# Compressed rows split ahead of a gate quarter and expanded behind it, and query pieces asked for five ahead

## The chip, the core and the metric

The kernel runs on one core of a Trainium2 chip. The metric is the device time of one execution in microseconds. Three runs of the kernel before took 1874.07, 1874.98 and 1877.89 us; the median is 1874.98.

## The reference

The reference is a two-layer backbone over 1024 latent tokens and 256 context tokens, 1024 wide, in float32. The even layer has four differential-attention heads and eight heads of multi-head latent attention, the odd layer a bidirectional mLSTM and neighbourhood attention. The change touches the even layer's projection and the start of its attention:

```python
z = jnp.einsum('bsd,de->bse', h, w_in) + b_in
q1, q2, k1, k2, v, cq, ckv, k_rope, gate = split_cols(z, EVEN_SPLIT)
...
qm = to_heads(jnp.einsum('bsr,re->bse', rms_norm(cq, q_norm_g), w_uq), MLA_HEADS)
kvm = to_heads(jnp.einsum('bsr,re->bse', rms_norm(ckv, kv_norm_g), w_ukv), MLA_HEADS)
q_nope, q_rope = qm[..., :MLA_NOPE], qm[..., MLA_NOPE:]
k_nope, vm = kvm[..., :MLA_NOPE], kvm[..., MLA_NOPE:]
...
y = jnp.concatenate([from_heads(oa), from_heads(ob)], axis=-1) * jax.nn.silu(gate)
```

So 256 columns of `z` are the compressed queries, 128 the compressed keys and values and 32 the rotary part of the keys. They are normalised by rows and expanded by `w_uq` and `w_ukv`. A further 1024 columns are the gate.

## The kernel before

A token group `TG` is four tiles of 128 tokens, four more, and the two tiles of context. A float32 product is made of three: each operand is split into a rounded high part and the rest, and `product` (L434 to L436) adds high by high, high by low and low by high in one PSUM bank. `parts` (L452, L453) makes such a split of a result: ScalarE writes the high part `eh`, VectorE the low part `el`, and each has two buffers. A buffer is free again when its store has landed.

The projection stage ends with this sequence. The 416 compressed columns are made for all tiles (L1270 on, the tile `cz`). Then `compressed(t0, n)` does for one group, in this order: the norms on GpSimd (L1291, L1296), the rotation of the key part, the transposes (L1306) and their splits into `cq` and `ck` (L1309, L1310), the rotary key part with its store to `s_kr` (L1317), four blocks of expanded keys with two stores each to `s_mk` (L1325), six blocks of expanded queries whose stores go to `s_mq` (L1338), and one block of values for each tile, stored to `s_mv` (L1360). A query block of the first four holds two heads and takes four stores; each of the last two holds sixteen columns of all eight heads and takes sixteen. All stores and loads are issued by SyncE's queue, one behind the other.

`gate(j)` makes a quarter of the gate: 256 columns for all three groups, 24 matmuls to a bank, a SiLU on ScalarE into the tile `e` (two buffers, shared with the values and the rotation), and a store (L1375). When it begins it takes its split weights, and at the same moment asks for the next quarter's (`next(w0)`, load L363, split L383 and L391, one staging buffer `raw`).

The four tiles of banks "tr" belong to the compressed rows, the four banks "mm" to the gate. Outside the parts that are marked as manual, the order of the instructions on each engine is set when the program is built: among those that are estimated to be ready, the one that stands earlier in the text goes first. So the order of the text gives precedence, and work from further on fills in.

When the pool `cp` of the compressed rows (it holds `uq`, `wu`, `cz`, `cq`, `ck`) is closed, the pool `a0` is opened on the same side of the memory, and the first attention unit's tiles are loaded into it: 24 loads of L590 to L592 for queries and keys, one for values (L597), one for the gate (L599). `gate(3)` stands behind that.

The attention has a plan written out by hand: each task has an engine, an estimated cost, the tasks before it, and the buffers that it takes and gives; `Plan.run` picks the task that can start earliest among the next 99. `Latent.shifts` adds the rough scores that give each row's maximum ahead of the latent heads (L858): for each head, nine steps of one or two tiles, which read query pieces of 256 tokens, `rq`, five buffers, loaded by L850. The key tiles for them go into the weight ring (L844, L845). One step goes behind each of the 36 blocks of the differential heads, and the rest are spread over the latent heads. In the kernel before, the load of a piece is added to the plan in the step that first uses it.

Of the kernel before, what the change touches and what calls it, by code (L numbers as in the profile page):

```python
# [19 lines left out]
P = 128  # L20
D = 1024
# [33 lines left out]
RQ = 5  # L55
# [146 lines left out]
def hybrid_kernel(ctx, tc, t, out, dbg=None):  # L202
# [253 lines left out]
    def keys_of(tt):  # L456
        k0 = 0 if tt < LT else LT
        return k0, NT - k0 * P
# [78 lines left out]
    def on_vector(n):  # L537
        return fixed["V"] + n / 960

    def on_scalar(n, act=True):  # L540
        return fixed["act" if act else "copy"] + n / 1200
# [10 lines left out]
                self.load_scores(pool, b)  # L552
            self.load_values(pool)

    spare, stored = {}, []

    def moves(plan, bank, dst, m, last, cut=3):

# [12 lines left out]
    def taken(key):  # L571
        return spare[key].pop(0)

    def given(key, x):
        spare[key].append(x)
# [234 lines left out]
    class Latent(Unit):  # L810
# [26 lines left out]
        def shifts(self, plan, a):  # L837


            x = {}  # L840

            def load(_):
                x["k"] = ring[0].tile([P, KT, WC], FR, name=("whi", "wlo")[a]).rearrange("p k n -> p (k n)")[:, :NT]
                dma(out=x["k"][0:64, :].bitcast(F32), in_=s_mk[0][self.p, 64 * a:64 * a + 64, :])  # L844
                dma(out=x["k"][64:96, :].bitcast(F32), in_=s_kr[0])  # L845

            def load_q(i):
                def emit(_):
                    x["q", i] = rough.tile([P, 256], FR, name="rq", bufs=RQ)
                    dma(out=x["q", i][0:96, :].bitcast(F32), in_=s_mq[0][2 * self.p + a][:, i * 256:(i + 1) * 256])  # L850
                return emit

            def cut(tt, c0, k0, n0, nn):
                def emit(_):
                    if c0 + n0 == 0:
                        x["s", tt] = taken("s")
                    s = x["s", tt if tt < LT else LT]
                    T.matmul(s[:, c0 + n0:c0 + n0 + nn], x["q", tt // 2][0:96, tt % 2 * P:tt % 2 * P + P],  # L858
                             x["k"][0:96, k0 * P + n0:k0 * P + n0 + nn], start=True, stop=True)
                return emit  # L860

            def top(tt, n):
                def emit(_):
                    if self.kept is None:
                        self.kept = at.tile([P, 2, TILES], F32, name="kept", bufs=2)
                    w = keys_of(tt)[1]
                    V.tensor_reduce(out=self.kept[:, a, tt:tt + n], in_=x["s", tt][:, :n * w].rearrange("p (m k) -> p m k", k=w),  # L867
                                    axis=AX.X, op=ALU.max, negate=True)
                    given("s", x["s", tt])
                return emit  # L870

            def turn(_):
                x["t"] = taken("tp")
                T.transpose(x["t"][0:2 * TILES, 0:P], self.kept.rearrange("p a t -> p (a t)"), ident)

            def rows(_):
                x["r"] = at.tile([P, 512], F32, name="yd", bufs=2)[:, :P]
                S.copy(out=x["r"][0:2 * TILES, :], in_=x["t"][0:2 * TILES, 0:P])
                given("tp", x["t"])

            def store(_):
                dma(out=s_sh[self.p].rearrange("a (t q) -> (a t) q", q=P), in_=x["r"][0:2 * TILES, :])

            def loading():
                x["ready"] = plan.add("D", 2.5, load, [], [f"r{a}"], rank=0)

            def step(tt, n):
                k0, w = keys_of(tt)
                if tt % 2 == 0:
                    x["loaded", tt // 2] = plan.add("D", 0.6, load_q(tt // 2), [], ["rq"], rank=0)  # L890
                last = [x["ready"], x["loaded", tt // 2]]
                cuts = [(tt + i, i * w, k0, n0, nn) for i in range(n) for n0, nn in key_cuts(w)]
                for i, c in enumerate(cuts):
                    freed = [f"r{a}"] * (tt + n == TILES) + ["rq"] * (n == 2 or tt % 2)
                    last = [plan.add("P", c[-1] / 2250, cut(*c), last, [] if i else ["s"],
                                     freed if i == len(cuts) - 1 else [], rank=-2e4 if i else RM)]
                self.shift.append(plan.add("V", on_vector(n * w), top(tt, n), last, [], ["s"], rank=RM))
                if tt + n == TILES and a == 1:
                    last = plan.add("P", 0.2, turn, self.shift, ["tp"])
                    last = plan.add("A", on_scalar(P, False), rows, [last], ["yd"], ["tp"])  # L900
                    self.rows = plan.add("D", 1.0, store, [last], [], ["yd"])
            return loading, [partial(step, tt, 1) for tt in range(LT)] + [partial(step, LT, 2)]

        def scores(self, plan, g):
# [150 lines left out]
    with space(name="pa", bufs=1) as pa, space(name="psa", bufs=1, space=PSUM) as psa0, ExitStack() as wa_stack:  # L1055
# [76 lines left out]
        with space(name="za", bufs=2) as za:  # L1132
# [70 lines left out]
            with space(name="rd", bufs=1) as rd:  # L1203
                table = rd.tile([P, 2, NLAT], F32, name="table")
                dma(out=table, in_=t["rope_da"])
                for j in range(4):
                    hi, lo = next(w0)
                    for g, (t0, n) in enumerate(TG):
                        sl = slice(t0 * P, (t0 + n) * P)
                        x = []  # L1210
# [33 lines left out]
            with space(name="cp", bufs=1, side="right") as cp:  # L1244
                uq = [cp.tile([P, 2, 768], FR, name=f"uq{i}") for i in range(2)]
                for a in range(3):
                    sl = slice(a * 256, (a + 1) * 256)
# [37 lines left out]
                def compressed(t0, n):  # L1285
                    sl = slice(t0 * P, (t0 + n) * P)
# [14 lines left out]
                    cq = [cp.tile([P, 2, 512], FR, name=f"cq{i}") for i in range(2)]  # L1301
                    ck = [cp.tile([P, 512], FR, name=f"ck{i}") for i in range(2)]
                    for a in range(3):
# [3 lines left out]
                        g = vt[0][:, V0["qg"] + a:V0["qg"] + a + 1] if a < 2 else vt[0][:, V0["kg"]:V0["kg"] + 1]  # L1307
# [7 lines left out]
                    pr = parts(za, ps[0:32, :n * P], 32, n * P)  # L1315
                    for i in range(2):
                        dma(out=s_kr[i][:, sl], in_=pr[i])  # L1317
                    for p in range(4):
                        ps = pst.tile([P, 512], F32, name="tr")
                        wsl = slice(p * P, (p + 1) * P)  # L1320
                        product(ps[:, :n * P], lambda k: wk[0][:, wsl], lambda k: wk[1][:, wsl],
                                lambda k: ck[0][:, :n * P], lambda k: ck[1][:, :n * P], 1)
                        pr = parts(za, ps[:, :n * P], P, n * P)
                        for i in range(2):
                            dma(out=s_mk[i][p, :, sl], in_=pr[i])  # L1325
# [14 lines left out]
                    x = []  # L1340
# [21 lines left out]
                def gate(j):  # L1362
                    hi, lo = next(w0)
                    for a in range(2):
                        f = 2 * j + a
                        for t0, n in TG:
                            sl = slice(t0 * P, (t0 + n) * P)
                            ps = psa.tile([P, 512], F32, name="mm")
                            product(ps[:, :n * P], lambda k: hi[:, k, a * P:(a + 1) * P],
                                    lambda k: lo[:, k, a * P:(a + 1) * P],  # L1370
                                    lambda k: hhi[:, k, sl], lambda k: hlo[:, k, sl])
                            e = za.tile([P, 512], F32, name="e")
                            S.activation(out=e[:, :n * P], in_=ps[:, :n * P], func=AF.Silu,  # L1373
                                         bias=vt[0][:, V0["eg"] + f:V0["eg"] + f + 1])
                            dma(out=s_gate[f, :, sl], in_=e[:, :n * P])  # L1375

                for g, tg in enumerate(TG):
                    compressed(*tg)
                    if g < 2:
                        gate(g)  # L1380
            gate(2)
            a0 = attn_stack.enter_context(space(name="a0", bufs=1, side="right"))
            units = [Differential(h) for h in range(4)] + [Latent(p) for p in range(4)]
            units[0].load(a0)
# [5 lines left out]
    def key_cuts(w):  # L1390
        return [(n0, min(512, w - n0)) for n0 in range(0, w, 512)]

    with space(name="a1", bufs=1, side="right") as a1, space(name="at", bufs=1, side="right") as at, \
# [43 lines left out]
        plan = Plan("attention", s=2, st=0, r0=1, r1=1, rq=RQ, p=NP, pt=NPT, tp=2, oo=2, raw=1, k00=0, k01=0, v0=0, k10=1, k11=1, v1=1, yd=2)  # L1437
# [25 lines left out]

        loaded(da[1])
        ahead = [u.shifts(plan, a) for u in mla for a in range(2)]
        for loading, _ in ahead[:2]:
            loading()
        parts_left = [(j, step) for j, (_, steps) in enumerate(ahead) for step in steps]
# [610 lines left out]
    with space(name="hidc", bufs=1, side="right") as hq, space(name="zt", bufs=2, side="right") as zt, \  # L2079
# [8 lines left out]
        for a in range(2):  # L2088
# [7 lines left out]
            for tt in range(TILES):  # L2096
                if a == 0 and tt == 0:
                    with space(name="xin1", bufs=6, side="right") as xp:
                        for t0, n in TG[1:]:
                            xs = []  # L2100
                            for i in range(n):
                                x = xp.tile([P, D], F32, name="xt")
# [16 lines left out]
        with space(name="cv", bufs=1, side="right") as cv:  # L2119
            for j in range(4):  # L2120
                w = next(w1)
                for a in range(2):
# [5 lines left out]
                    for tg in TG[:2 if f < 4 else 3]:  # L2128
                        ps, sl, n = feature(w, a, tg, psa)
# [10 lines left out]
                    n = NLAT if f < 4 else NT  # L2140
# [7 lines left out]
        plan = Plan("mlstm", kt=2, qt=2, ve=1, ew=1, ktok=1, vw=6, cs=1, nd=1, ho=2, ml=5, mm=3, e=2, hv=2, zv=2, bb=2, raw=1)  # L2148
# [30 lines left out]
        for j in range(2):  # L2179
# [7 lines left out]
            for tt in range(TILES):  # L2187
# [5 lines left out]
                def store(_, x, j=j, tt=tt):  # L2193
# [3 lines left out]
                done, x = products(plan, 256, (ah, al, lambda k, w=w: w[0][:, k, :256], lambda k, w=w: w[1][:, k, :256]),  # L2197
                                   ready)
# [23 lines left out]
    with space(name="nf", bufs=1, side="right") as nf, space(name="psf", bufs=1, space=PSUM) as psf:  # L2222
# [246 lines left out]
        plan = Plan("neighbours", s=2, tp=2, mm=2, np=4, npt=2, eo=2, e=2, hv=2, raw=1, wr=1, unit=2, kl=1, bt0=1, bt1=1, slot=0, y=2, nyy=1)  # L2469
# [132 lines left out]
```

## Time and profile before

| | |
|---|---|
| median of three runs | 1874.98 us |
| the profiled execution | 1873.51 us |
| its span, first to last instruction | 1871.8 us |
| mean granted TensorE clock | 0.976 |
| TensorE, busy | 1740.0 us, 93% |
| VectorE, busy | 1115.5 us, 60% |
| ScalarE, busy | 727.1 us, 39% |
| GpSimd, busy | 584.6 us, 31% |
| DMA, mean over the span | 146 GB/s |

In the profile, PE is TensorE's matmuls and PEld its weight loads, DVE is VectorE, ACT ScalarE, POOL GpSimd, and SPq the queue of SyncE, which issues every DMA. A row of the list of instructions gives start, duration, engine, line, operation, the tile written and the tiles read, the size, the number of instructions, and in brackets the idle time before it with what ended it. Matmuls overlap, so their pace is read from the starts. In the rows of waits, the numbers are the time in total, how often, and the longest.

### The profile page before, as it was taken

How to read it: one execution, taken by the hardware profiler on the slowest of the kernel's cores; microseconds unless marked ns; L12 is line 12 of the kernel's file. 1: busy time of each engine (PE TensorE's matmuls, PEld its weight loads, DVE VectorE, ACT ScalarE, POOL GpSimd, SP SyncE). 2: the span in 40 equal slices, each digit the busy share in tenths (PEclk: the TensorE clock that was granted, in tenths of full speed). 3: DMA queues.
4: the chain of work that ended last, by engine and by line, in shares of the span. 5: the costliest groups of instructions: out<-in, count | busy, mean ns of one | idle time of the engine just before them, and what ended most of it. 6: DMA issues, size and time to landing. Idle time of an engine off the chain costs nothing.

```text
span 1871.8 us, 28143 instructions
## 1 busy us (share of the span) xinstructions
PE 1740.0 (93%) x10354; PEld 1436.3 (77%) x10354; DVE 1115.5 (60%) x1959; ACT 727.1 (39%) x1466; POOL 584.6 (31%) x534
## 2 busy tenths in 40 slices
PE   6999998998988899999999989999889989998898
PEld 3878996787877786566567878888889877876786
DVE  3743224212887887878868644755775125667855
ACT  2422132323765664445523122325543233444521
POOL 1422242111334435567534412210110002223544
PEclk9999998999999999999999989999999999999999
DMA  9777315659426525245163342227432376667642
GB/s 347 229 236 263 113 55 152 174 168 233 100 60 146 131 64 142 85 98 151 59 212 130 103 145 68 95 77 219 162 101 75 110 227 157 177 173 191 201 145 89
DMA packets 203697, 274.19 MB, mean 146 GB/s; under 512 B 21256, under 2 KB 155160, under 8 KB 203304
## 3 DMA queue, kind: packets, MB, share of 16 engines
q1 hardware_dynamic: 203560, 272.39, 49.7%
q8 instruction: 82, 1.34, 0.3%
q14 instruction: 55, 0.45, 0.1%
HBM read 195.33 MB, written 77.00 MB: 145 GB/s over the span
## 4 chain that ended last, share of the span: by engine, by line
PE 69%; DVE 10%; DMA 8%; SPq 4%; issue 4%; ACT 3%; POOL 2%; DVEq 0%; POOLq 0%; ACTq 0%
PE mm L434 9%; PE mm L436 9%; PE mm L435 9%; PE tp L952 4%; SPq L1338 3%; PE tp L650 3%; PE mm L2014 3%; PE mm L2015 3%; PE mm L2016 2%; PE st L916 2%; PE st L918 2%; PE st L917 2%; PE s L858 2%; PE s L612 2%; PE tp L2447 1%
## 5 line engine op out<-in xcount | busy, mean ns | idle before, releaser
L391 POOL TENSOR_TENSOR wlo<-raw,whi 128x1024 fp32r<-128x1024 f32 (+2 forms) x38 | 92.9, 2444 | 257.9 <-ACT whi L383 254.6
L1402 DVE TENSOR_REDUCE nm<-s 128x1 f32<-128x1280 f32 x64 | 94.3, 1488 | 66.1 <-PE s L613 65.1
L434 PE MATMUL mm<-hhi,whi 128*128 128x512 f32 (+1 forms) x352 | 123.8, 353 | 3.6 <-ACT e L1373 2.9
L2404 POOL TENSOR_SCALAR np<-np,nrz 128x640 f32<-128x640 f32 x64 | 53.0, 832 | 231.7 <-DVE nrz L2401 208.7
L436 PE MATMUL mm<-hhi,wlo 128*128 128x512 f32 (+1 forms) x352 | 123.4, 351 | 0.3 <-POOL wlo L391 0.3
L435 PE MATMUL mm<-hlo,whi 128*128 128x512 f32 (+1 forms) x352 | 123.5, 351 | 0.0
L867 DVE TENSOR_REDUCE kept<-s 128x1 f32<-128x1280 f32 (+1 forms) x72 | 100.4, 1395 | 14.7 <-PE s L858 13.5
L383 ACT CAST whi<-raw 128x1024 fp32r<-128x1024 f32 (+2 forms) x54 | 55.9, 1035 | 135.9 <-PE mm L436 55.0
L1409 ACT ACTIVATE p<-s,nm 128x1280 f32<-128x1280 f32 x64 | 84.9, 1328 | 28.1 <-DVE nm L1402 24.9
L612 PE MATMUL s<-o 128*128 128x512 f32 (+1 forms) x192 | 74.7, 390 | 14.0 <-ACT p L1409 8.3
L2014 PE MATMUL mm<-h,whi 128*128 128x512 f32 x192 | 78.1, 407 | 3.3 <-DVE hv L2050 3.3
L635 POOL TENSOR_SCALAR p<-p,ratio 128x512 f32<-128x512 f32 x32 | 31.9, 997 | 153.4 <-DVE ratio L627 135.8
L650 PE MATMUL tp<-v,pt 128*128 128x128 f32 x640 | 77.9, 280 | 0.9 <-ACT pt L564 0.9
L434 PEld LDWEIGHTS mm<-hhi,whi 128*128 128x128 f32 x352 | 66.3, 189 | 14.4 <-ACT e L1373 3.5
L650 PEld LDWEIGHTS tp<-v,pt 128*128 128x128 f32 x640 | 75.9, 196 | 1.8 <-ACT pt L564 1.4
L2015 PE MATMUL mm<-h,whi 128*128 128x512 f32 x192 | 76.0, 396 | 0.0
L932 ACT ACTIVATE pt<-st 128x512 f32<-128x512 f32 (+1 forms) x88 | 50.3, 578 | 66.0 <-PE st L918 57.3
L2016 PE MATMUL mm<-h,wlo 128*128 128x512 f32 x192 | 75.8, 395 | 0.0
L2397 ACT ACTIVATE np<-np,nnm 128x640 f32<-128x640 f32 x64 | 52.9, 827 | 56.0 <-DVE nnm L2391 51.8
L436 PEld LDWEIGHTS mm<-hhi,wlo 128*128 128x128 f32 x352 | 66.5, 189 | 9.7 <-POOL wlo L391 0.5
L434 PE MATMUL mm<-whi,hhi 128*128 128x256 f32 (+1 forms) x240 | 73.6, 307 | 0.0
L435 PEld LDWEIGHTS mm<-hlo,whi 128*128 128x128 f32 x352 | 66.6, 189 | 9.1
(470 smaller groups left out, 5337.0 us busy)
## 6 DMA issues: line engine op xcount, KB each, us to landing
adaw<-in_ada_w_dram SPq DMA_DIRECT2D x16, 1024.0 KB
raw<-in_od_w_in_dram SPq DMA_DIRECT2D x32, 512.0 KB
o<-s_qk SPq DMA_DIRECT2D x96, 160.0 KB
bt<-in_bias_tables_dram SPq DMA_DIRECT2D x16, 576.0 KB
adaw<-in_ada_dram SPq DMA_DIRECT2D x16, 512.0 KB
o<-s_mq SPq DMA_DIRECT2D x16, 480.0 KB
raw<-in_ev_w_in_dram SPq DMA_DIRECT2D x12, 512.0 KB
s_gate<-e SPq DMA_DIRECT2D x24, 256.0 KB
```

The lines of the kernel that those rows point to most:

```text
L391: (eng or self.eng).tensor_tensor(out=lo, in0=self.raw, in1=hi, op=ALU.subtract)
L434: T.matmul(ps, ahi(k), bhi(k), start=k == k0, stop=False)
L435: T.matmul(ps, ahi(k), blo(k), start=False, stop=False)
L436: T.matmul(ps, alo(k), bhi(k), start=False, stop=k == nk - 1)
L612: T.matmul(s[:, n0:n0 + nn], ql, self.kh[b][:, ks], start=True, stop=False)
L650: T.matmul(o[:, :P], x["pt"][:, c, :], self.v[:, k0 + c, :], start=c == 0, stop=c == nch - 1)
L867: V.tensor_reduce(out=self.kept[:, a, tt:tt + n], in_=x["s", tt][:, :n * w].rearrange("p (m k) -> p m k", k=w), axis=AX.X, op=ALU.max, neg ...
L1402: V.tensor_reduce(out=nm, in_=s[:, :w], axis=AX.X, op=ALU.max, negate=True)
L1409: S.activation(out=p[:, :w], in_=s[:, :w], func=AF.Exp, bias=nm, accum_out=z)
L2014: T.matmul(ps, ah, bh, start=k == 0, stop=False)
L2015: T.matmul(ps, ah, bl, start=False, stop=False)
L2016: T.matmul(ps, al, bh, start=False, stop=k == KT - 1)
```

## The change

`compressed` is cut in two behind the store of the rotary key part. What stands before the cut keeps its name and returns `cq` and `ck`; what stands behind is `expanded`. For every group the order is now: `compressed`, the quarter of the gate with the group's number, `expanded`. Before, the order was `compressed` whole, then the quarter; and the third quarter stood behind the closing of the pool. Nothing is added to the computation or taken from it.

For the query pieces, the loads become a list of 40 requests, five for each head. The first five are put in the plan ahead of everything but the second unit's loads. Each later one is added at the start of a step that gives a piece's buffer back (the odd tiles, and the step of two tiles), so that it stands five pieces ahead of its use.

```diff
-    spare, stored = {}, []
+    spare, stored, asked = {}, [], []
...
+            def asking(i):
+                x["loaded", i] = plan.add("D", 0.6, load_q(i), [], ["rq"], rank=0)
+
             def step(tt, n):
                 k0, w = keys_of(tt)
-                if tt % 2 == 0:
-                    x["loaded", tt // 2] = plan.add("D", 0.6, load_q(tt // 2), [], ["rq"], rank=0)
+                if (tt % 2 or n == 2) and asked:
+                    asked.pop(0)()
                 last = [x["ready"], x["loaded", tt // 2]]
...
+            asked.extend(partial(asking, i) for i in range(5))
             return loading, [partial(step, tt, 1) for tt in range(LT)] + [partial(step, LT, 2)]
...
                     for i in range(2):
                         dma(out=s_kr[i][:, sl], in_=pr[i])
+                    return cq, ck
+
+                def expanded(t0, n, cq, ck):
+                    sl = slice(t0 * P, (t0 + n) * P)
                     for p in range(4):
...
                 for g, tg in enumerate(TG):
-                    compressed(*tg)
-                    if g < 2:
-                        gate(g)
-            gate(2)
+                    c = compressed(*tg)
+                    gate(g)
+                    expanded(*tg, *c)
             a0 = attn_stack.enter_context(space(name="a0", bufs=1, side="right"))
...
         ahead = [u.shifts(plan, a) for u in mla for a in range(2)]
+        for ask in asked[:RQ]:
+            ask()
+        del asked[:RQ]
         for loading, _ in ahead[:2]:
             loading()
```

## The prediction

> **What bounds the kernel now.** I read the page's busy times first, then the even layer's projection stretch by stretch, then its chain, its waits and the two queues concerned.
>
> ```profile
> span 1871.8 us, 28143 instructions
> ...
> PE 1740.0 (93%) x10354; PEld 1436.3 (77%) x10354; DVE 1115.5 (60%) x1959; ACT 727.1 (39%) x1466; POOL 584.6 (31%) x534
> ```
>
> TensorE is busy for 93% of the span, so an edit pays only where it closes a hole in TensorE or restores its clock. The changed stage runs from about 276 us (first compressed rows) to 450 us (first scores). The stretches below hold its holes; the columns after the times are length, then busy time and count for PE, PEld, DVE, ACT, POOL, then the granted clock, DMA share and GB/s.
>
> ```profile
> 313.00:332.00 19.00, 10.06 (x36) 6.68 (x35) 5.59 (x8) 6.17 (x10) 0.00 (x0) 0.64 0.55 168
> ...
> 369.00:383.00 14.00, 10.28 (x56) 8.06 (x55) 4.41 (x10) 7.17 (x16) 2.38 (x1) 1.00 0.81 269
> ...
> 409.00:429.00 20.00, 17.24 (x88) 14.10 (x87) 0.00 (x0) 5.69 (x8) 4.79 (x2) 1.00 1.02 275
> 429.00:450.00 21.00, 20.47 (x110) 17.56 (x108) 0.00 (x0) 3.67 (x6) 0.00 (x0) 1.00 0.89 233
> ```
>
> TensorE idles 8.94 + 3.72 + 2.76 + 0.53 = 16.0 us, and in the first of these it also runs at a granted clock of 0.64. Why it idles there, by the waits and the chain of 276 to 452:
>
> ```profile
> by line: SPq L1338 32.8%; PE mm L436 9.5%; PE mm L434 9.2%; PE mm L435 9.0%; issue 7.0%; DMA raw<-in_ev_w_in_dram 3.6%; PE tr L434 3.1%; DMA o<-s_qk 3.0%; PE tr L436 2.9%; PE tr L435 2.8%; DMA s_mv<-e 2.8%; POOL wlo L391 1.4%; DVE el L453 1
> ```
>
> ```profile
> DVE el L453 <- DMA s_mq<-el: 26.0, 11, 7.0
> ...
> PE tr L434 <- DVE el L453: 6.9, 2, 6.0
> ```
>
> A third of the chain is SyncE issuing the small query stores of L1338. They hold the two buffers of each split part (`eh`, `el`), the split of the next rows waits for them, the PSUM bank stays full, and TensorE stands:
>
> ```profile
> 327.04 0.79 PE L434 MATMUL tr<-ck,wu 128*128 128x512 f32 x1 [6.01 <-DVE el L453]
> 327.63 0.63 PE L435 MATMUL tr<-ck,wu 128*128 128x512 f32 x1
> 328.05 0.63 PE L436 MATMUL tr<-ck,wu 128*128 128x512 f32 x1
> ```
>
> Matmuls start 0.42 us apart there (327.63 to 328.05) instead of the 0.23 worked out below, some 16 of them before the clock is back: 3 us more. So a stage in which TensorE never waited would reach the scores at 450.08 - 16.0 - 3 = 431 us. That is the floor.
>
> **The change, part by part.** First TensorE's work, from start times:
>
> ```profile
> 360.97 0.28 PE L434 MATMUL mm<-hhi,whi 128*128 128x256 f32 x1
> ...
> 363.84 0.40 PE L434 MATMUL mm<-hhi,whi 128*128 128x512 f32 x1
> ```
>
> ```profile
> 369.31 0.60 PE L1306 MATMUL tr<-cst,cz 128*128 128x128 f32 x4
> ...
> 373.19 0.35 PE L434 MATMUL tr<-ck,wu 128*128 128x256 f32 x1 [1.63 <-DVE e L447]
> ```
>
> Between the first pair lie 24 products of 256 columns: 2.87 us, 0.12 each. From 363.84 to 369.31 lie 24 of 512: 5.47 us, 0.23 each. A quarter of the gate is twice (5.47 + 5.47 + 2.87) = 27.6 us. Expanding a group of four tiles is 60 products of 512 columns, 14.0 us; the last group, of two tiles, has 48 of 256 and 6 of 512, 7.2 us. None of this is removed; the change only orders it.
>
> **Splitting ahead, expanding behind.** The transposes and splits of a group (L1306 to L1317) now stand before 27.6 us of gate products, so their chain on ScalarE and VectorE is covered, and the stores of one group have those 27.6 us to drain before the next group wants the same buffers. I cost the 6.01 us hole, the slow clock behind it and the smaller holes at group changes as gone, less 1.5 us left over (bounds: 0, and 6.0 if one such hole returns elsewhere). The first weights of the last gate quarter also move ahead of the last group's stores; before, they were queued behind them, with the tail of the stage behind the weights:
>
> ```profile
> 409.78 0.40 SPq L363 DMA_DIRECT2D raw<-in_ev_w_in_dram  x1
> 410.27 0.51 SPq L590 DMA_DIRECT2D o<-s_qk  x1
> ...
> 430.94 0.30 SPq L592 DMA_DIRECT2D o<-s_qk  x1
> ```
>
> **What is late next.** The last group is now expanded behind the third gate quarter instead of ahead of it, so only 7.2 + 27.6 = 34.8 us of TensorE work follow its start. Call that start T0: 431 - 34.8 + 1.5 = 397.7 us. After T0 SyncE must issue all of that group's stores, and behind them, because the tiles of the first attention unit take the place of the weights that the expansion reads, that unit's 24 pieces:
>
> ```profile
> L1338 SPq DMA_DIRECT2D s_mq<-eh x24: 364/418/595, 381.9 to 406.7; - x24
> L1338 SPq DMA_DIRECT2D s_mq<-el x24: 364/418/1299, 386.1 to 408.0; - x24
> ```
>
> ```profile
> 374.70 0.50 SPq L1325 DMA_DIRECT2D s_mk<-eh  x1
> ...
> 378.14 0.39 SPq L1375 DMA_DIRECT2D s_gate<-e  x1
> ...
> 391.12 3.60 SPq L1338 DMA_DIRECT2D s_mq<-eh  x8
> 394.82 3.60 SPq L1338 DMA_DIRECT2D s_mq<-el  x8
> 398.51 1.09 SPq L1338 DMA_DIRECT2D s_mq<-eh  x2
> 399.70 1.18 SPq L1338 DMA_DIRECT2D s_mq<-el  x2
> ```
>
> Eight small stores take 394.82 - 391.12 = 3.70 us, 0.46 each; those that go in pairs 0.6 to 0.64 each. With 32 of the first kind, 16 of the second, 8 stores of key parts and 2 of values that is 40 x 0.4625 + 16 x 0.64 + 1.1 = 29.8 us. They begin 374.70 - 373.19 = 1.5 us after T0, and four gate stores in between cost 4 x 0.47 = 1.9 us. For the unit's pieces I take the second unit's, issued with nothing else in the queue:
>
> ```profile
> 450.87 0.38 SPq L590 DMA_DIRECT2D o<-s_qk  x1
> ...
> 465.65 0.30 SPq L592 DMA_DIRECT2D o<-s_qk  x1
> ```
>
> ```profile
> 589.04 0.30 SPq L850 DMA_DIRECT2D rq<-s_mq  x1
> ```
>
> ```profile
> 592.33 1.40 PE L858 MATMUL s<-whi,rq 96*128 96x512 f32 x3 [3.55 <-DMA rq<-s_mq]
> ```
>
> That is 14.8 us from the first to the last, and 3.3 us from an issue to the product that uses it. The second scores can start at 397.7 + 1.5 + 29.8 + 1.9 + 14.8 + 3.3 = 449.0 us, and the first scores, which need half of the pieces, some 7 us before them. TensorE would be ready at about 433, so most of the 19 us is given back to this wait. Against before:
>
> ```profile
> 451.35 0.40 PE L612 MATMUL s<-o 128*128 128x512 f32 x1
> ...
> 454.54 0.50 PE L612 MATMUL s<-o 128*128 128x512 f32 x1 [1.87 <-ACT p L1409]
> ```
>
> The second scores come 2.35 us sooner. The 1.87 us wait behind them, for the exponentials of the first scores, is then over already: 2.35 + 1.87 = 4.2 us for the stage. Bounds: 19 us if the pieces come in time, and 7.7 us lost in the slow rival below.
>
> What the waiting TensorE does to its clock, by the same start before:
>
> ```profile
> 456.00:460.00 4.00, 2.21 (x9) 1.47 (x9) 3.85 (x6) 2.40 (x3) 0.54 (x1) 1.00 1.05 218
> 460.00:464.00 4.00, 3.30 (x15) 2.69 (x16) 3.96 (x6) 1.81 (x7) 1.96 (x2) 0.63 1.03 214
> 464.00:468.00 4.00, 4.00 (x14) 3.32 (x13) 1.58 (x3) 0.84 (x2) 1.97 (x2) 0.52 1.04 216
> ```
>
> It drops to 0.63 and 0.52 for 8 us after a stretch that is half idle, and I leave that cost in the sum unchanged: before pays it too. [...]
>
> **Query pieces five ahead.** Two holes are at stake:
>
> ```profile
> PE s L858 <- DMA rq<-s_mq: 4.3, 2, 3.6
> ```
>
> ```profile
> 563.24 0.30 SPq L590 DMA_DIRECT2D o<-s_qk  x1
> ...
> 586.60 0.30 SPq L592 DMA_DIRECT2D o<-s_qk  x1
> ```
>
> The late piece was issued right behind a whole unit's 24 pieces (563.24 to 586.60), so its place in the queue made it late, not the lack of a buffer: the five buffers hold the pieces of nine steps. Asked for nine steps ahead, it goes in front. The bounds are 0 and 4.3 us; I take 3.0, since VectorE and ScalarE are behind by then and some of the hole returns as a wait for them. Each ask now waits for a buffer as soon as the plan thinks it free, and SyncE with it; behind it stand the next unit's pieces and the stores of `yd`:
>
> ```profile
> SPq L850 <- PE s L858: 46.0, 10, 8.9
> ```
>
> Such waits are there already, up to 8.9 us, and the pieces behind them are used tens of us later (unit two's, issued from 450.87, after the nine blocks of unit one), so I cost them at nothing; without that cover one costs up to 8.9 us. The first five asks also go ahead of the two key tiles of L844 and L845 and wait for the last gate product, whose operands lie where they are put: 5 x 0.46 = 2.3 us in front of tiles that are needed after the first scores.
>
> The sum: 4.2 + 3.0 = 7.2 us. The profiled execution took 1873.51 us (its span of 1871.8 and 1.7 around it), so 1866.3. The median of the three runs is 1874.98, 1.5 above it: **1867.8**.
>
> **The rivals.**
>
> The pieces come in time: TensorE reaches the last group early, because full gate banks make it take those products first, and the loads end before the gate does. For it: TensorE already mixes gate and expansion products. Against it: the first unit's loads need the expansion finished in any order. 19 + 4.3 us less: 1850.2 + 1.5 = 1851.7.
>
> The order doesn't become the engines' order: each engine's order in this stage is set when the kernel is compiled, by what is estimated to be ready, and TensorE's list already has gate products between those of one expansion. Then only the query pieces count: 3.0 us, 1872.0, within 0.2%.
>
> The slow one: SyncE at the end of the stage. With one hole of 6.0 us left, T0 is 403.7, and the unit's pieces go at their old pace, 410.27 to 430.94, 20.7 us, beside gate stores. The second scores start at 403.7 + 1.5 + 29.8 + 1.9 + 20.7 + 3.3 = 460.9, 9.55 late, less 1.87: 7.7 us lost, 3.0 regained, 1873.5 + 4.7 + 1.5 = 1879.7. It decides from T0 = 401.9 for the stage (397.7 + 4.2) and from 404.9 for the kernel at the quick pace. For it speaks that SyncE and its loads have 51 us of work after T0 and TensorE 35.
>
> **How the numbers follow.** Forecast 0.50 (its own range 1862 to 1871), in time 0.12, order unchanged 0.20, slow 0.18. A measurement of this kernel tells about 0.2%, 3.7 us. Faster 0.62, within 0.20, slower 0.18. The range takes in the greater part of the early case and the slow one: 1856 to 1880.
>
> **What would show it.** Right: no hole above 3 us between 300 and 395, clock 1.00 there; the last group's first product near 398; SyncE without a pause from there to the unit's last piece near 446; TensorE waiting for `o<-s_qk` at the first scores; no wait of L858 for `rq`. Wrong: last-group products before 390, or scores starting at 432 without a wait, would show the loads hidden; gate products after the expansion of their group would show the order unmoved; new holes of L612 or L858 would show the plan upset by the earlier asks.

## The result, and the profile after

The kernel became slower: 1891.60 us, the median of four runs (1886.90 to 1894.84), against 1874.53 of the kernel before in four runs. The ratio is 1.0085, with a 95% interval of 1.0067 to 1.0104. The profiled execution took 1890.1 us. The forecast was 1867.8 us with a range of 1856 to 1880, so it missed both the sign and the range.

The busy times on the page of the kernel after:

```profile
span 1888.4 us, 28161 instructions
...
PE 1736.4 (92%) x10354; PEld 1434.8 (76%) x10354; DVE 1116.9 (59%) x1959; ACT 727.2 (39%) x1466; POOL 583.5 (31%) x534
```

Hardly any engine has more to do than before (VectorE 1.4 us, ScalarE 0.1): TensorE is even 3.6 us below its old 1740.0. The span is 16.6 us longer, so TensorE idles 20.2 us more. TensorE's list of instructions says where:

```profile
349.75 0.80 PE L434 MATMUL tr<-ck,wu 128*128 128x512 f32 x1 [6.46 <-DVE el L453]
...
393.23 0.28 PE L434 MATMUL tr<-ck,wu 128*128 128x256 f32 x1
...
469.24 0.79 PE L612 MATMUL s<-o 128*128 128x512 f32 x1 [23.69 <-ACT e L1381]
...
471.54 0.63 PE L612 MATMUL s<-o 128*128 128x512 f32 x1
```

The last row of these answers to the second scores of before, at 451.35: they come 20.2 us later. The first scores, at 450.08 before, come 19.2 us later, behind one hole of 23.69 us. From the first scores to the end of the span it is 1888.4 − 469.24 = 1419.2 us, and it was 1871.8 − 450.08 = 1421.7. So the loss is made in the changed stage, and it is paid in that hole. The hole of 6.01 us at 327.04 that the change was costed to remove has also returned, as 6.46 at 349.75.

The three stretches of the stage with the largest holes now (columns as in the prediction; another 5.1 us of idle time lies between 376 and 416):

```profile
336.00:356.00 20.00, 13.54 (x52) 10.27 (x51) 4.23 (x7) 5.90 (x10) 0.00 (x0) 0.83 0.58 182
...
436.00:456.00 20.00, 8.61 (x48) 7.44 (x48) 0.00 (x0) 1.38 (x2) 0.00 (x0) 0.86 1.04 214
456.00:476.00 20.00, 5.86 (x18) 4.61 (x18) 2.98 (x2) 5.51 (x8) 0.00 (x0) 0.55 0.92 253
```

From 436 to 476 TensorE is busy for 14.5 of 40 us while the DMA engines are full (a share of 1.04 and 0.92). The hole is put down to ScalarE's tile `e` (the SiLU of the gate, now L1381), so ScalarE's list is next:

```profile
437.24 0.69 ACT L1381 ACTIVATE e<-mm,vt 128x512 f32<-128x512 f32 x1 [0.35 <-DMA s_mv<-e]
461.64 0.47 ACT L1381 ACTIVATE e<-mm,vt 128x256 f32<-128x256 f32 x1 [23.71 <-DMA s_gate<-e]
462.32 0.69 ACT L1381 ACTIVATE e<-mm,vt 128x512 f32<-128x512 f32 x1 [0.21 <-DMA s_gate<-e]
468.10 1.09 ACT L1381 ACTIVATE e<-mm,vt 128x512 f32<-128x512 f32 x2 [5.09 <-DMA s_gate<-e]
```

Each of these SiLUs waits for one of the two buffers of `e`, and a buffer is free when its store (to `s_mv` in the first row, to `s_gate` in the others) has landed: the gate stores issued from 453.58 on take 7.8 us to landing, the median, and the SiLU behind them starts at 461.64. SyncE's list, before and then after, says why the stores are late:

```profile
289.04 0.34 SPq L1325 DMA_DIRECT2D s_mk<-eh  x1
```

```profile
308.38 0.81 SPq L1333 DMA_DIRECT2D s_mk<-eh  x2
...
435.08 0.38 SPq L590 DMA_DIRECT2D o<-s_qk  x1
...
451.14 0.30 SPq L592 DMA_DIRECT2D o<-s_qk  x1
...
453.58 1.13 SPq L1383 DMA_DIRECT2D s_gate<-e  x2
455.51 4.15 SPq L850 DMA_DIRECT2D rq<-s_mq  x5
...
463.42 6.19 SPq L1383 DMA_DIRECT2D s_gate<-e  x4
```

The reader is to see three things. The first key store is 19.3 us later than before (308.38 against 289.04), since 27.6 us of gate products now stand ahead of the first expansion. The unit's first piece, issued when the stores are done, is 24.8 us later (435.08 against 410.27). And two stores of the last gate quarter stand behind all 26 loads of the unit, the next ones behind five query pieces and the key tiles as well. The DMA view of the same stretch (433 to 471) gives for the store its count, size and the median time from issue to landing:

```profile
s_gate<-e SPq DMA_DIRECT2D x4, 256.0 KB, 7.8
```

The place of these stores in the queue is not new. In the kernel before, the last quarter's first store (435.59) also stands behind the 26 loads, and a SiLU waits for it:

```profile
445.41 0.48 ACT L1373 ACTIVATE e<-mm,vt 128x256 f32<-128x256 f32 x1 [11.09 <-DMA s_gate<-e]
```

```profile
450.08 0.50 PE L612 MATMUL s<-o 128*128 128x512 f32 x1 [0.61 <-ACT e L1373]
```

There it is hidden: TensorE has products until the first scores and waits for `e` for 0.61 us only. What is new is that the loads come 24.8 us later, and TensorE's products end at 445.5.

The chain of 430 to 472 shows the two parts that make up the wait, loads of pieces and stores of the gate:

```profile
by line: DMA o<-s_qk 31.5%; DMA s_gate<-e 29.5%; SPq L1346 9.6%; SPq L591 6.2%; PE s L612 4.4%; SPq L590 4.0%; issue 3.4%; SPq L592 3.0%; PE s L613 2.5%; ACT e L1381 2.5%; SPq L1368 2.5%; SPq L845 1.4%; SPq L844 1.1%; ACTq L1381 0.1%; SPq L
```

### The profile page after: what moved, and what is told of

Read it like the earlier page. It is cut to its first block, busy times and chain, and to the rows that moved or that the text cites. A ratio compares the mean times of both kernels' runs of the same rounds, so it can differ in the third digit from the quotient of the medians.

```text
span 1888.4 us, 28161 instructions
## 1 busy us (share of the span) xinstructions
PE 1736.4 (92%) x10354; PEld 1434.8 (76%) x10354; DVE 1116.9 (59%) x1959; ACT 727.2 (39%) x1466; POOL 583.5 (31%) x534
## 4 chain that ended last, share of the span: by engine, by line
PE 69%; DVE 11%; DMA 7%; issue 4%; SPq 3%; ACT 3%; POOL 2%; DVEq 0%; ACTq 0%; POOLq 0%
PE mm L434 8%; PE mm L435 8%; PE mm L436 8%; PE tp L956 4%; PE tp L650 3%; PE mm L2024 3%; PE mm L2025 3%; PE mm L2026 3%; SPq L1346 2%; PE st L920 2%; PE st L922 2%; PE st L921 2%; PE s L612 2%; PE s L858 2%; DVE nm L1409 2%
## 5 line engine op out<-in xcount | busy, mean ns | idle before, releaser
L867 DVE TENSOR_REDUCE kept<-s 128x1 f32<-128x1280 f32 (+1 forms) x72 | 100.5, 1395 | 14.5 <-PE s L858 13.2
L434 PEld LDWEIGHTS mm<-hhi,whi 128*128 128x128 f32 x352 | 66.8, 190 | 14.8 <-ACT e L1381 4.8
L612 PEld LDWEIGHTS s<-o 128*128 128x128 f32 x192 | 37.0, 192 | 49.4 <-ACT e L1381 23.9
```

The lines of the kernel that those rows point to most:

```text
L434: T.matmul(ps, ahi(k), bhi(k), start=k == k0, stop=False)
L612: T.matmul(s[:, n0:n0 + nn], ql, self.kh[b][:, ks], start=True, stop=False)
```

## The experiments

Theory A: the end of SyncE's queue is the cause. The unit's pieces come late, and the last gate quarter's stores behind them hold `e`, so PSUM banks aren't emptied and the scores can't start. Theory B, its rival: the early query pieces, which stand ahead of the last gate stores, make the wait. Theory D came up when A missed: what counts is how late SyncE begins with the stores of expanded rows, since from there on its queue is one long chain. Ratios are against the kernel before on the same chip, with a 95% interval.

### The two parts of the change, alone

The split of `compressed`, with the query pieces asked for as before:

```diff
-                if (tt % 2 or n == 2) and asked:
-                    asked.pop(0)()
+                if tt % 2 == 0:
+                    x["loaded", tt // 2] = plan.add("D", 0.6, load_q(tt // 2), [], ["rq"], rank=0)
...
-        for ask in asked[:RQ]:
-            ask()
-        del asked[:RQ]
```

> The split alone, query pieces asked for in the step of their use as before. Theory A (the end of the projection stage: the last gate stores stand in SyncE's queue behind the first attention unit's 26 loads, the SiLUs wait for their tile, the first scores for the PSUM banks that the SiLUs empty): nearly all of the loss stays, first scores at 463 to 470 us, time 1884 to 1891, and the two rq holes of 4.3 us are back. Theory B (the five asks and four key tiles that stand in front of the last gate stores make the loss): time at or under 1878, first scores before 457.

Measured: 1894.96 us, ratio 1.0123 (1.0096 to 1.0151), 4.0 us above the range of A.

The early query pieces, with the order of before:

```diff
                 for g, tg in enumerate(TG):
                     c = compressed(*tg)
+                    expanded(*tg, *c)
-                    gate(g)
-                    expanded(*tg, *c)
+                    if g < 2:
+                        gate(g)
+            gate(2)
```

> The asks alone, group order of before. Theory A: first scores at 450 to 452 us as before, no rq hole, 2 to 3 us saved: 1871 to 1873. Theory B: the five asks delay the first scores here too, to 455 or later, and the time is 1876 or more.

Measured: 1873.67 us, ratio 0.9997 (0.9977 to 1.0018). The first scores of the two kernels:

```profile
466.88 0.80 PE L612 MATMUL s<-o 128*128 128x512 f32 x1 [22.89 <-ACT e L1381]
```

```profile
449.31 0.50 PE L612 MATMUL s<-o 128*128 128x512 f32 x1 [0.61 <-ACT e L1381]
```

The whole loss belongs to the split: without the early pieces the hole is still 22.89 us, and B falls. Their place in the queue is worth at most the 2.4 us between 469.24 and 466.88. The early pieces alone make no difference that the medians show; what they do in the trace is told further below.

### The gate stores behind the loads

The SiLU tiles of the last quarter get buffers of their own for the second and third group, so that no SiLU waits for one of the late stores:

```diff
-                        for t0, n in TG:
+                        for g, (t0, n) in enumerate(TG):
...
-                            e = za.tile([P, 512], F32, name="e")
+                            e = za.tile([P, 512], F32, name=("e", "z0", "z1")[g] if j == 3 else "e")
```

> The changed kernel, but each SiLU of the last gate quarter writes a tile of its own (names e, z0, z1 with two buffers each), so that none waits for a store. Theory A: the first scores wait only for their own pieces, whose last issue for the first half was at 441 and for the second at 451: first scores at 447 to 450, second at 455 to 459, time 1875 to 1879. Rival C (the pieces themselves are what is late, the SiLUs only end last): first scores stay within 3 us of 469 and the time within 3 us of 1890.

Measured: 1882.62 us, ratio 1.0052 (1.0033 to 1.0072). First and second scores, and the first rough scores:

```profile
447.76 0.77 PE L612 MATMUL s<-o 128*128 128x512 f32 x1 [3.85 <-DMA o<-s_qk]
...
457.30 0.77 PE L612 MATMUL s<-o 128*128 128x512 f32 x1 [6.89 <-DMA o<-s_qk]
...
469.14 1.41 PE L858 MATMUL s<-whi,rq 96*128 96x512 f32 x3 [4.89 <-DMA whi<-s_kr]
```

The scores came where A put them, and the wait is now for the pieces and no longer for `e`. The span is 1888.4 − 1877.8 = 10.6 us shorter. The time missed A's 1875 to 1879 by 3.6 us. The third row shows a wait that A hadn't counted: the key tiles of L844 and L845, asked for behind the unit's loads and the five query pieces, hold TensorE for 4.89 us.

The same from the other side: the unit's loads are written behind the last gate quarter, so that the gate stores go in front of them.

```diff
-            units[0].load(a0)
             gate(3)
+            units[0].load(a0)
```

> The changed kernel with the first unit's loads written behind the last gate quarter, so that its stores go ahead of them in SyncE's queue. Theory A: no SiLU waits for a store behind 26 loads; the scores wait for their pieces alone: first at 446 to 451, second at 456 to 462, time 1878 to 1885, as with the gate's own tiles. Rival C (the pieces themselves, not the SiLUs): first scores within 3 us of 469, time over 1887.

Measured: 1882.13 us, ratio 1.0033 (1.0012 to 1.0054).

```profile
450.02 0.76 PE L612 MATMUL s<-o 128*128 128x512 f32 x1 [3.40 <-DMA o<-s_qk]
...
459.76 0.77 PE L612 MATMUL s<-o 128*128 128x512 f32 x1 [7.27 <-DMA o<-s_qk]
```

Two ways of freeing `e` give the same scores within 2.5 us and remove the wait for ScalarE. So the gate stores' place is a cause, and about half of the loss (0.33 to 0.52 of 0.85% remain). The other half remains: the pieces themselves are late.

### Why the pieces are late

The third gate quarter goes behind the last expansion again, while the first two stay ahead of theirs:

```diff
                     c = compressed(*tg)
-                    gate(g)
+                    if g < 2:
+                        gate(g)
                     expanded(*tg, *c)
+            gate(2)
```

> The changed kernel, but the third gate quarter stands behind the last group's expansion, as before the change; the first two groups stay split around their quarters. Theory A: 27.6 us of gate products lie again between the last group's start and the scores, SyncE has its stores out before the last quarter, and the first scores come at 440 to 452: time 1862 to 1875. Rival C' (the loss comes from the split of the first two groups): new holes between 340 and 400, time stays over 1882.

Measured: 1889.64 us, ratio 1.0091 (1.0073 to 1.0110). A missed. SyncE's first piece, a SiLU and the product behind it:

```profile
429.45 0.39 SPq L590 DMA_DIRECT2D o<-s_qk  x1
```

```profile
430.63 0.69 ACT L1381 ACTIVATE e<-mm,vt 128x512 f32<-128x512 f32 x1 [6.85 <-DMA s_mv<-e]
```

```profile
431.37 0.80 PE L434 MATMUL mm<-hhi,whi 128*128 128x512 f32 x1 [14.73 <-ACT e L1381]
```

With 27.6 us of products taken away from in front of the last expansion, the first piece came only 435.08 − 429.45 = 5.6 us sooner. TensorE instead stood for 14.73 us in the gate, because the values, which use `e` too, wait in SyncE's queue behind the query stores. What this kernel still shares with the changed one is the late start: its first key store is at 310.10. That is theory D. To test it, the first group is expanded at once, and only the later splits go ahead of a quarter:

```diff
-                for g, tg in enumerate(TG):
-                    c = compressed(*tg)
+                c = compressed(*TG[0])
+                expanded(*TG[0], *c)
+                for g in range(2):
+                    c = compressed(*TG[g + 1])
                     gate(g)
-                    expanded(*tg, *c)
+                    expanded(*TG[g + 1], *c)
+            gate(2)
```

> The changed kernel, but the first group is expanded at once, ahead of the first gate quarter; the second group is split ahead of the first quarter and expanded behind it, the third around the second quarter; the third quarter stands behind the pool's end as before. Theory D (SyncE's small stores are the stage's chain, and the change leaves SyncE without them from 289 to 308 us while the first quarter runs): first key store at 289 to 291, the unit's first piece asked for at 408 to 416 instead of 435, first scores at 440 to 452, time 1862 to 1875. Rival E (a quarter between split and expansion is what costs, wherever the first store falls): the unit's pieces stay later than 425, first scores later than 460, time over 1882.

Measured: 1874.10 us, ratio 0.9994 (0.9979 to 1.0009). SyncE's first key store and first piece, then TensorE:

```profile
288.76 0.34 SPq L1333 DMA_DIRECT2D s_mk<-eh  x1
...
412.24 0.51 SPq L590 DMA_DIRECT2D o<-s_qk  x1
```

```profile
326.82 0.79 PE L434 MATMUL tr<-ck,wu 128*128 128x512 f32 x1 [6.75 <-DVE el L453]
...
452.84 0.50 PE L612 MATMUL s<-o 128*128 128x512 f32 x1 [0.61 <-ACT e L1381]
```

The first store is back, 19.6 us sooner than in the changed kernel; the first piece comes 22.8 us sooner, and the whole loss is gone. (The scores missed the expected 440 to 452 by 0.8.) From the first key store to the first piece it is 410.27 − 289.04 = 121.2 us in the kernel before, 126.7 in the changed one, 119.3 with the third quarter behind and 123.5 here: the stretch is about as long wherever it begins. This run also takes a quarter away from in front of the second expansion, so it doesn't test the first store alone. The hole at the group change is still there, 6.75 us: splitting ahead of the gate doesn't remove it, whether the first store stands at 308.38 or at 288.76.

### Making SyncE's chain shorter

If SyncE's chain sets the pieces, fewer stores should pay in both kernels. The first attempt stores a whole block of query rows, two heads or eight, with one DMA:

```diff
-                            for h in range(P // w):
-                                dma(out=s_mq[b][h0 + h, r0:r0 + w, sl], in_=pr[b][w * h:w * h + w, :])
+                            dma(out=s_mq[b][h0:h0 + P // w, r0:r0 + w, sl], in_=pr[b])
```

In the changed kernel:

> The changed kernel, with each query block's part stored by one DMA for all its heads instead of two or eight: 12 issues a group instead of 48. Theory D: a group keeps SyncE for 10 to 14 us instead of 29, so the unit's first piece is asked for at 405 to 415 instead of 435, first scores at 430 to 446, time 1855 to 1871. Rival F (the bytes and their landing bound the stage, not the issues): the pieces stay later than 428 and the time over 1882.

In the kernel before:

> The kernel before with the same merged stores. Theory D: the 6.0 us hole near 327 goes, the unit's first piece is asked for before 400, first scores at 430 to 442, time 1856 to 1868. Rival F: first scores within 3 us of 450, time within 4 us of 1874.

Measured: 1950.57 us, ratio 1.0401 (1.0373 to 1.0429), and 1947.75 us, ratio 1.0383 (1.0358 to 1.0409). D missed by far in both. The waits of the first (time, how often, the longest), one issue on SyncE, and one stretch:

```profile
DVE el L453 <- DMA s_mq<-el: 88.2, 12, 13.2
```

```profile
339.38 6.42 SPq L1345 DMA_DIRECT2D s_mq<-el  x1
```

```profile
300.00:345.00 45.00, 33.26 (x150) 27.01 (x148) 8.13 (x11) 9.32 (x15) 7.30 (x4) 0.89 0.32 110
```

There are fewer issues, but one of them keeps SyncE for up to 6.42 us (0.46 for a small one), and the split waits 88.2 us for the buffer that the stores hold (27.2 in the changed kernel), with the DMA engines busy for 0.32 of this stretch. The second attempt leaves the first four blocks alone and makes two stores of the sixteen of each of the last two blocks (one for the high part, one for the low), with sixteen entries in the outermost dimension; no run so far had shown whether that counts. For that the rotary columns of the weights are laid out column by column, each with its eight heads:

```diff
-    rope_da, rope_mla = turned(64, 4), turned(32, 8)
+    rope_da, rope_mla = turned(64, 4), np.repeat(turned(32, 1), 8, axis=0)
...
-    order = np.concatenate([heads[:, 0:64].reshape(-1), heads[:, 64:80].reshape(-1), heads[:, 80:96].reshape(-1)])
+    order = np.concatenate([heads[:, 0:64].reshape(-1), heads[:, 64:80].T.reshape(-1), heads[:, 80:96].T.reshape(-1)])
...
+                            if f >= 4:
+                                dma(out=s_mq[b][:, r0:r0 + w, sl].rearrange("h r n -> r h n"), in_=pr[b])
+                                continue
```

In the changed kernel:

> The changed kernel, with the rotary columns laid out by column first, so that each of the last two query blocks is stored by one DMA for each part whose outermost dimension is sixteen long, instead of eight small ones; the other stores are as they were. A group issues 32 - 4 = 28 stores less. Theory D (issues are the chain): 40 x 0.46 + 16 x 0.64 + 1.1 becomes 12 x 0.46 + 10.2 + 1.1 = 17 us a group instead of 30, so the last group's stores end 10 to 14 us sooner, the unit's first piece is asked for at 416 to 424 instead of 435, first scores at 446 to 458, time 1872 to 1882. Rival F (landing, not issue): landings of these stores are over 6 us as in the run with all heads in one store, the time is over 1890.

In the kernel before:

> The kernel before with the same two merged stores. Theory D: the 6.0 us hole near 327 goes, SyncE reaches the first unit's pieces at 375 to 400 instead of 410, first scores at 432 to 443, time 1856 to 1868. Rival F: holes of 5 us or more behind these stores, first scores at 450 or later, time 1872 or more.

Measured: 1876.33 us, ratio 1.0014 (0.9999 to 1.0029), and 1860.07 us, ratio 0.9923 (0.9906 to 0.9941). The scores of the first, and the merged low-part stores of its first two groups (count, size, median time to landing):

```profile
448.73 0.80 PE L612 MATMUL s<-o 128*128 128x512 f32 x1 [21.34 <-ACT e L1384]
```

```profile
s_mq<-el SPq DMA_DIRECT2D x4, 256.0 KB, 2.9
```

The second: the stretch of the old hole, SyncE's first piece, and the first scores:

```profile
300.00:345.00 45.00, 42.43 (x204) 34.27 (x203) 21.62 (x29) 20.36 (x32) 7.74 (x5) 1.00 0.79 225
```

```profile
396.88 0.40 SPq L590 DMA_DIRECT2D o<-s_qk  x1
```

```profile
435.63 0.50 PE L612 MATMUL s<-o 128*128 128x512 f32 x1 [0.61 <-ACT e L1376]
```

D holds in both kernels. In the kernel before, SyncE is done with the stores 410.27 − 396.88 = 13.4 us sooner, TensorE has its full clock (1.00) through the old hole, and the scores come 14.5 us sooner. In the changed kernel the pieces are 21.2 us sooner (413.92 against 435.08, and sooner than the 416 to 424 expected); what stays is the gate stores' wait, 21.34 us. But issuing is not the whole of SyncE's stretch. From the first key store (289.00 and 308.63) to the first piece it is now 107.9 and 105.3 us, 13.3 and 21.4 less than with the old stores, while 84 issues fewer at 0.46 us would be 38.6 us, an estimate. What else holds the stretch wasn't tried. Two runs more tell whether either part of the change is worth something once the chain is short. The early query pieces on the order of before:

> The same as the run before it, with the query pieces asked for five ahead. Theory D, with the asks worth what they were alone (2 to 4 us of holes in the attention): 1853 to 1867, 1 to 4 us under the run without them. Rival: the asks give nothing here, within 1 us of it.

And the changed kernel with its own SiLU tiles for the last quarter, as above:

> The changed kernel with both repairs: the last two query blocks in one store for each part, and a tile of its own for each SiLU of the last gate quarter. Theory A and D together: TensorE's work ends near 427 as in the run with the merged stores, the scores wait for their pieces alone, first at 427 to 430, second at 434 to 439, time 1856 to 1865; the split and the old order, given the same merged stores (1860 and 1861), then come out within 4 us of one another. If the split has a worth of its own once both waits are gone: under 1856. If something else of the split costs: over 1868.

Measured: 1861.46 us, ratio 0.9931 (0.9911 to 0.9952), and 1862.79 us, ratio 0.9941 (0.9918 to 0.9964). The second scores of the latter:

```profile
434.81 0.76 PE L612 MATMUL s<-o 128*128 128x512 f32 x1 [6.39 <-DMA o<-s_qk]
```

Neither beats 1860.07, and the intervals overlap; the 1 to 4 us expected of the early pieces didn't show. The kernel before with the sixteen-row stores beats both kernels of the study, and the change adds nothing to it that can be told.

## Why the prediction was wrong

The prediction's chain can be followed link by link, in us of the profiled execution. The fourth line is the kernel with its own SiLU tiles, where only the pieces are waited for.

| link | forecast | measured | late by |
|---|---|---|---|
| last group's first product, T0 | 397.7 | 393.23 | −4.5 |
| unit's first piece asked for | 430.9 | 435.08 | 4.2 |
| unit's last piece asked for | 445.7 | 451.14 | 5.4 |
| second scores, held by pieces alone | 449.0 | 457.30 | 8.3 |
| second scores | 449.0 | 471.54 | 22.5 |
| end of the span | 1864.6 | 1888.4 | 23.8 |

**The gate stores are the step that failed: 14.2 us** (471.54 − 457.30). The prediction counted gate stores once, as four "in between" that cost 1.9 us, and it named no store of the last quarter behind the unit's loads. They aren't only time in the queue. A store that is late holds `e`, `e` holds a SiLU, the SiLU holds a PSUM bank, and the scores want the banks: the SiLU waited 23.71 us for the store, and the first scores 23.69 us for the SiLU. The prediction had all the links in front of it: the two buffers of `e`, the one queue, and in the kernel before a SiLU's wait of 11.09 us for such a store. Two experiments that cut the chain at different links brought the scores back to 457.30 and 459.76.

**The pieces came 8.3 us later than worked out.** Of this 4.5 us is the stores (the first piece at 435.44 in that kernel), 1.3 the pace of the pieces (16.1 us for 24 instead of 14.8), and 2.5 from the last issue to the product (5.8 us instead of 3.3). The price of 29.8 us for the stores was worked out behind T0 alone. SyncE, though, didn't come to T0 with an empty queue: value stores of the group before were still issued at 393.73 and 396.99, and six gate stores, not four, stood between. T0 was taken as the start of the chain, and its value was nearly right, but the reason was not. T0 is 2.4 us sooner in the kernel with the third quarter behind (390.88), which lost just as much; what brought the time back was the kernel whose stores start at 288.76 again.

**The 6.0 us hole did not go.** It was costed as gone less 1.5 us, with its return as the bound. The prediction said that the split's chain is covered by 27.6 us of gate products. ScalarE's list shows why there are no gate products to cover it:

```profile
345.32 0.60 ACT L452 ACTIVATE eh<-tr 128x512 fp32r<-128x512 f32 x1 [6.29 <-DMA s_mq<-el]
...
350.43 0.58 ACT L445 COPY e<-tr 128x512 f32<-128x512 f32 x1 [4.51 <-DMA s_mv<-e]
...
353.35 1.27 ACT L1381 ACTIVATE e<-mm,vt 128x512 f32<-128x512 f32 x2 [1.05 <-DVE el L453]
```

In this list a high part that waits for the query stores and a value copy that waits for `e` stand ahead of the gate's SiLUs. No SiLU starts between 307.40 and 353.35, and in that time TensorE finishes four banks of gate products, the last at 341.23; the four gate banks are full, and TensorE has nothing to take. In the sum this cost nothing by itself, since T0 came 4.5 us ahead of its forecast all the same (TensorE left 8.3 us of the third quarter's products for behind it), and SyncE was the later one. That T0 came near its forecast was luck: one hole too many, and products left over.

**The early query pieces gave 1.1 to 2.5 us, where 3.0 us were taken, and by another path than the one costed.** The wait of L858 for `rq` did go in every kernel that asks early. The stretch between the same two score products, 94 matmuls, first before with its second hole, then after with its holes:

```profile
585.10:604.63 19.53, 14.95 (x94) 13.68 (x92) 14.24 (x17) 8.62 (x28) 6.65 (x10) 0.83 0.38 93
604.63 0.50 PE L612 MATMUL s<-o 128*128 128x512 f32 x1 [1.03 <-DVE kept L867]
```

```profile
603.97:621.20 17.23, 12.98 (x94) 11.43 (x92) 14.17 (x17) 8.98 (x30) 6.68 (x10) 1.00 0.43 105
608.64 0.50 PE L858 MATMUL s<-whi,rq 96*128 96x512 f32 x1 [0.98 <-ACT p L1416]
612.53 0.38 PE L650 MATMUL tp<-v,pt 128*128 128x128 f32 x1 [0.82 <-DVE yd L793]
615.83 0.41 PE L1433 MATMUL tp<-cst,p 128*128 128x128 f32 x2 [0.80 <-DVE p L638]
621.20 0.50 PE L612 MATMUL s<-o 128*128 128x512 f32 x1 [1.65 <-DVE kept L867]
```

Before, the holes are 3.55 (the row at 592.33 in the prediction) + 1.03 = 4.58 us; after, 0.98 + 0.82 + 0.80 + 1.65 = 4.25. So the wait for the piece came back as waits for VectorE and ScalarE, which are behind in this stretch. The prediction expected that for some of the hole; it was nearly all. But the granted clock is 1.00 instead of 0.83, and TensorE is busy for 12.98 us instead of 14.95 with the same work. The stretch is 2.3 us shorter: the changed kernel is 18.9 us late ahead of it and 16.6 behind it, as at the end of the span. Three pairs of profiles differ by the early pieces alone: the stretch takes 19.53 and 17.00 us on the order of before, 18.35 and 17.23 with the split, 18.27 and 16.83 with the sixteen-row stores; the clock is 0.83 to 0.91 without them and 1.00 with them. The medians can't show so little, with runs of one kernel up to 15.6 us apart (1862.23 to 1877.87 with the early pieces alone).

Also costed at nothing were SyncE's waits for a piece's buffer, 46.0 us before. They are 178.1 now, the longest 15.8, and no loss follows: the kernel is as late at the end as at 621.20. And the five pieces ahead of the key tiles were costed at nothing. In the kernels whose scores start early, with 4.89 and 4.08 us of wait for `s_kr`, that cover was gone. Whether the pieces or the unit's loads ahead of them made those tiles late wasn't tried.

**What held.** The work of no engine grew by more than 1.4 us. The first scores do wait behind SyncE's loads, the third group's expansion does start near 398 (393.23), and the slow rival named the place and the sign. Its price of 1879.7 us was 11.9 too low, because it too priced pieces alone. Its condition, T0 from 401.9 on, was wrong: the loss came with T0 at 393.23. The clock was not a large term. The first 20 us from the first scores on, after and before:

```profile
469.00:489.00 20.00, 16.25 (x73) 13.31 (x74) 14.27 (x15) 10.13 (x17) 4.47 (x4) 0.79 0.76 172
```

```profile
450.00:470.00 20.00, 15.56 (x73) 12.62 (x73) 14.29 (x15) 9.93 (x17) 4.46 (x4) 0.83 0.98 211
```

The granted clock is 0.79 behind a hole of 23.69 us and 0.83 without one: (0.83 − 0.79) x 20 = 0.8 us, an estimate from these two rows.

## What to carry to other kernels

When one queue issues all transfers, ask first when its chain of stores begins and what stands at its end: here work moved ahead of the first store (19.3 us later) was paid again at the unit's last load (451.14 against 430.94, 20.2 us later). Follow each store that stands behind a row of loads to the buffer that it holds, and on through the engine that waits for the buffer to the PSUM bank, before pricing it by its issue time; ask what hides its wait today. Where a wait is to be removed in a stretch in which two other engines are nearly behind, price the waits for them that can come in its place: here 4.58 us of holes became 4.25. Compare the whole stretch, clock included (19.53 us at 0.83 became 17.23 at 1.00), and not the holes alone.

## What was not expected of the hardware

One DMA in place of several wasn't cheaper by itself. With two or eight heads as the outermost dimension the kernel before went from 1874.67 to 1947.75 us; with sixteen rows outermost, for the last two blocks alone, from 1874.23 to 1860.07; in the changed kernel such a store of 256 KB landed in 2.9 us, the median. The DMA shares from 300 to 345 us were 0.24 with the two- and eight-headed stores against 0.79 with the sixteen rows on the order of before, and 0.32 against 0.64 on the changed one. Why the one form cost so much and the other didn't isn't shown: the runs don't part the two-headed store from the eight-headed one, and no view here shows how many engines one store used.
